# A Trainium2 encoder block: the softmax's sums of exponentials as products of f16 halves instead of fp32

## The chip, the cores and the metric

The kernel runs on one core of a Trainium2 chip. A core has five engines, each with its own instruction queue worked off in order: TensorE (PE; its weight loads are listed apart as PEld), VectorE (DVE), ScalarE (ACT), GpSimd (POOL) and SyncE (SP, which only issues DMAs). They share SBUF; TensorE's products go to PSUM, which POOL does not reach. The metric is the device time of one execution, in microseconds.

## What is computed

One layer of an encoder block, on two batches of 2048 tokens with 1024 features and the same weights. The part that matters here is the attention: 8 query heads in 2 groups (kv heads), head size 64, every query against all 2048 keys.

```python
def one_block(qblk):
    s = jnp.einsum('bkgqd,bskd->bkgqs', qblk, k).astype(jnp.float32) * scale
    pr = jax.nn.softmax(s, axis=-1).astype(v.dtype)
    return jnp.einsum('bkgqs,bskd->bqkgd', pr, v)
...
a = _blocked_gqa(q, k, v) * jax.nn.silu(ga)
fo = _fourier_branch(f, w_fmix) * jax.nn.silu(gf)
h = h + jnp.concatenate([a, fo], axis=-1) @ w_out
gate = jax.nn.sigmoid(_rmsnorm(h, g_ple) @ w_ple_gate)
return h + (p @ w_ple) * gate
```

The softmax is done as exponentials of the scores less their maximum, summed over the keys; the products with V are divided by the sums at the end.

## The kernel before

**Stages.** First the projections of both batches (until about 820 us of the profiled span), then a long stage in which attention and a filler run interleaved (until about 2592 us), then what is left of the filler. The filler is the Fourier branch and after it the output projection, the gate and the final norm of tile after tile of 128 tokens.

**Units and steps.** Attention goes by 64 units: one of two batches, one of two kv heads, one of 16 blocks of 128 queries. The four heads of a kv head and 128 queries make 512 columns. A unit has 8 steps, each with 256 of the 2048 keys. Step `g` belongs to unit `g // 8`, and `j = g % 8` is its number in the unit. In a step:

- `scores(u, j)` issues six f16 products (L1166) into two PSUM banks `ps_s` that the unit keeps, two more in its first step, and then two exponentials on ACT (L1169) into the tile `p` of the tag `p32`, of which there are seven buffers. POOL adds `p` to the running sum `acc` of the unit (L1172 at step 1, L1174 at steps 2 to 7): 128x1024 in fp32. At step 7 POOL folds the two halves of `acc` into one of 128x512 (L1176).
- `lead(g)` issues the products for the row maxima of a unit that comes later (L1193, into the one buffer of `ps_m`) and their reduction on DVE (L1201); at every step 3 also `nm` on ACT (L1211).
- At step 4, `sums(u - 1, ...)` sums the folded `acc` of the unit before over its partitions, by products with a tile of ones on PE (L1244): two fp32 products of 256 columns, side by side in the two column halves of the array. `divide` then takes the reciprocal in PSUM (L1251) and multiplies (L1252) on DVE.
- At steps 0 and 4, behind all that, `pv` issues the fp32 products of four steps' exponentials with V (L1229). A step with such products gets no filler work; every other step gets about as much as a budget allows.

**Order.** PE, ACT, DVE and SP work in the order in which the program issues (`manual_schedule`); the order on POOL is planned by the framework, with its own costs. What is given to `defer` is issued at the start of the next step, in `flush`, ahead of that step's scores and reductions; other filler work is issued where it stands, at the end of its step. So the filler's DVE work of step 3 (such as L1407, which adds a product in PSUM to `h`) comes ahead of what was deferred in step 3, and that ahead of the reduction of step 4:

```python
self.flush()
u, j = g // 8, g % 8
...
    scores(u, j)
self.drain(lead(g))
if j == 4:
    ...
        sums(u - 1, ps[:, 0:256])
        divide(u - 1, ps[:, 0:256])
```

The filler's lines that the prediction names: L1481 (its products, two halves of the rows side by side), L1407, L1531 and L1535 (the two f16 halves `h_hl` of the normalised rows, by ACT and then by DVE), L1502 (squares), and the `rsh` chains (an inverse square root by tiny instructions, mostly on POOL). L390 and L393 are the two f16 halves of a weight, by ACT and DVE, in the first stage. L1051 is in the Fourier branch.

Of the kernel before, what the change touches and what calls it, by code (L numbers as in the profile page):

```python
# [11 lines left out]
F16 = mybir.dt.float16  # L12
I32 = mybir.dt.int32
AF = mybir.ActivationFunctionType
ALU = mybir.AluOpType
# [23 lines left out]
FIRST, SLOW = 30, 0.85  # L39
LAG = 3  # L40
P32 = 7
WHOLE = 2 * NT - 2
STOPS = (6, 9, 12, 15, 18)
MB = 2
# [96 lines left out]
class Build:  # L141
# [848 lines left out]
    def fourier2(self, pool, hook):  # L990
# [82 lines left out]
        for t in range(16):  # L1073
            if t == 10:
# [4 lines left out]
            fT = (pool.tile([128, 4, 2, 128], F32, name="fT", bufs=2) if t >= FP else  # L1079
                  self.att.tile([128, 4, 2, 128], F32, name="fT", tag="p32", bufs=P32))  # L1080
            fx = None
# [42 lines left out]
    def attention(self, kvp):  # L1124
# [3 lines left out]
        nc, st = self.nc, self.st  # L1128
        units = self.unit_order()
        n = len(units)  # L1130
        last = {units[u][:2]: u for u in range(n)}
        kt, vt, Q, P, O, MX, ACC, AT, M4, S, MR = {}, {}, {}, {}, {}, {}, {}, {}, {}, {}, {}

        def load_kv(s, kv):
            for b in range(2):
                k = kvp.tile([128, 4, 3, 128], F16, name=f"k{kv}", bufs=2)
                for h in range(2):
                    nc.sync.dma_start(k[:, 2 * h:2 * h + 2], self.kTd[s][kv][:, 4 * b + 2 * h:4 * b + 2 * h + 2])
                kt[s, kv, b] = k
            for b in range(2):  # L1140
                v = kvp.tile([128, 8, 64], F32, name=f"v{kv}", bufs=2)
                nc.sync.dma_start(v[:], self.vd[s][kv][:, 8 * b:8 * b + 8])
                vt[s, kv, b] = v

        def load_q(u):
            s, kv, t = units[u]
            q1, q2 = [(pool if u > 2 else kvp).tile([128, 4, 128], F16, name=f"q{b}" if u > 2 else f"q{b}_0",
                                                    bufs=3) for b in (1, 2)]
            src = self.qTd[s][t][:, 4 * kv:4 * kv + 4, :]
            for b, q in enumerate((q1, q2)):  # L1150
                for y in range(2):
                    nc.sync.dma_start(q[64 * y:64 * y + 64], src[64 * b:64 * b + 64])
            Q[u] = q1, q2

        def scores(u, j):
            s, kv, t = units[u]
            P[u, j] = p = pool.tile([128, 2, 512], F32, name="p32", bufs=P32)
            k = kt[s, kv, j // 4]
            todo = [] if j else [(kone, MR.pop(u))]
            todo += [(k[:, j % 4, y], Q[u][b]) for y, b in ((1, 0), (1, 1), (2, 0))]  # L1160
            if j == 0:
                S[u] = [self.psS.tile([128, 512], F32, name="ps_s") for e in range(2)]
            for i, (w, q) in enumerate(todo):
                for e in range(2):
                    sl = slice(64 * e, 64 * e + 64)
                    nc.tensor.matmul(S[u][e][:], w[sl], q[sl].rearrange("p h q -> p (h q)"), start=j == i == 0,  # L1166
                                     stop=i + 1 == len(todo), skip_group_check=True)
            for e in range(2):
                nc.scalar.activation(p[:, e, :], S[u][e][:], AF.Exp, scale=self.sc["s_scale"][:])  # L1169
            if j == 1:  # L1170
                ACC[u] = pool.tile([128, 2, 512], F32, name="acc", bufs=2)
                nc.gpsimd.tensor_tensor(out=ACC[u][:], in0=P[u, 0][:], in1=p[:], op=ALU.add)  # L1172
            elif j > 1:
                nc.gpsimd.tensor_tensor(out=ACC[u][:], in0=ACC[u][:], in1=p[:], op=ALU.add)  # L1174
            if j == 7:
                nc.gpsimd.tensor_tensor(out=ACC[u][:, 0, :], in0=ACC[u][:, 0, :], in1=ACC[u][:, 1, :], op=ALU.add)  # L1176
                del Q[u], S[u]
                if u == last[s, kv]:
                    for b in range(2):
                        del kt[s, kv, b]  # L1180

        def maxima(u, k, first=False):

            s, kv, t = units[u]
            h, half = k // 2, k % 2
            if first:
                ps = [self.psX.tile([128, 512], F32, name="ps_x")[:] for _ in range(2)]
            else:
                pm = self.psM.tile([128, 1024], F32, name="ps_m")
                ps = [pm[:, c * 512:(c + 1) * 512] for c in range(2)]  # L1190
            for c in range(2):
                sl = slice(64 * c, 64 * c + 64)
                nc.tensor.matmul(ps[c], Q[u][0][sl, h, :], kt[s, kv, half][sl, :, 0, :], start=True, stop=True)  # L1193
            if k == 0:
                MX[u] = st.tile([128, 4, 2, 2 if first else 1], F32, name="a_mx", tag=f"a_mx{int(first)}", bufs=2)
                if first:
                    nc.gpsimd.memset(MX[u][:], -3e38)
            if first:
                yield
            for c, x in enumerate(ps if first else [pm[:]]):  # L1200
                nc.vector.reduce_max(MX[u][:, h, half, c:c + 1], x, axis=AX.X)  # L1201
            if k < 7:
                return
            mx = MX.pop(u)
            m = st.tile([128, 4], F32, name="a_m4", bufs=2)
            nc.vector.tensor_reduce(out=m[:], in_=mx[:].rearrange("p h a b -> p h (a b)"), op=ALU.max, axis=AX.X)
            M4[u] = m

        def negate(u):
            m = M4.pop(u)  # L1210
            nc.scalar.activation(nm[:].rearrange("p h (e c) -> p e h c", e=2)[:, :, :, 0],  # L1211
                                 m[:].unsqueeze(1).to_broadcast([128, 2, 4]), AF.Copy, scale=-1.0 / K_ONE)

        def max_rows(u):

            MR[u] = mr = kvp.tile([128, 4, 128], F16, name="mr", bufs=1)
            nc.sync.dma_start_transpose(mr[:], nm[:].rearrange("p h c -> p (h c)"))
# [20 lines left out]

        def sums(u, ps):

            acc = ACC.pop(u)
            av = acc[:, 0, :].rearrange("p (c e q) -> p e c q", e=2, q=128)
            for e in range(2):
                nc.tensor.matmul(ps[64 * e:64 * e + 64], self.ones[:], av[:, e], start=True, stop=True)  # L1244

        def divide(u, r):

# [21 lines left out]
        def lead(g):  # L1269

            v, k = divmod(g + AHEAD, 8)
            if v < n:
                yield from maxima(v, k, g < 0)
            if k == 1 and 0 <= v - 1 < n:
                negate(v - 1)
# [11 lines left out]
        pool = yield  # L1287
        self.ones = pool.tile([128, 64], F32, name="ones", bufs=1)
        nc.gpsimd.memset(self.ones[:], 1.0)
        fresh = {last[0, kv]: kv for kv in range(2)}  # L1290
        for g in range(8 * n + 7):
            self.step = g
            self.flush()
            u, j = g // 8, g % 8
            if j == 0 and 0 < u and u + 2 < n:
                load_q(u + 2)
            if j == 4 and u - 1 in fresh:
                load_kv(1, fresh[u - 1])
            if 0 <= u < n:
                scores(u, j)  # L1300
            self.drain(lead(g))
            if j == 4:
                if u + 1 < n:
                    max_rows(u + 1)
                if u > 0:
                    ps = self.bank()
                    sums(u - 1, ps[:, 0:256])
                    divide(u - 1, ps[:, 0:256])
            heavy = (g - 1) % PVG == PVG - 1 and 0 <= g - 1 < 8 * n
            if heavy:  # L1310
                self.run_slow(1 if j else 2)
                pv((g - 1) // 8, (g - 1) % 8 - PVG + 1)
            yield 0 if heavy else RATE if g >= 8 * n // 2 else 1 if g > FIRST else SLOW
# [39 lines left out]
    def outp(self, pool0, ow, open_pool):  # L1353
# [208 lines left out]
        def along(g, pr):  # L1562

            for us in g:
                for _ in range(round(us / 0.648) if us else 0):
                    next(pr, None)
                poll()
                yield us
# [59 lines left out]
        for t in range(N2 + 2):  # L1628
            pr = prep(t + 1) if ok(t + 1) else iter(())
            if ok(t):  # L1630
                yield from along(slot(out1(t, 0), t >= WHOLE), pr)
                if t == 1:
                    yield from middle(0)
                yield from along(slot(out1(t, 1), t >= WHOLE), pr)
                load_p(t)
                M.pop(t)
            if ok(t - 1):
                yield from wait(tk, t - 1)
                yield from along(slot(out3(t - 1, 0), t >= WHOLE), pr)
            if t:  # L1640
                yield from middle(t)
            if ok(t - 1):
                yield from along(slot(out3(t - 1, 1), t >= WHOLE), pr)
            if ok(t + 1):
# [226 lines left out]
```

## Time and profile before

| | |
|---|---|
| median of 3 runs | 2668.47 us (2668.46 to 2668.82) |
| the profiled execution: time, span | 2671.73 us, 2670.0 us |
| PE busy | 2611.3 us (98%) |
| DVE, ACT, POOL busy | 1612.9 (60%), 1184.7 (44%), 1630.1 us (61%) |
| granted TensorE clock, mean | 0.995 |
| the sums (L1244): records, mean of one | 256, 404 to 405 ns |
| POOL's adds (L1174): number, mean of one | 384, 2394 ns |

The profile shows one execution. A busy share is the time in which an engine had an instruction under way. A matrix product in fp32 stands in the profile as two records. In a list of one line's instructions, three numbers with strokes between them are the shortest, the median and the longest duration in ns. A time in brackets behind a row of a timeline is the idle time of that engine ahead of it, with what ended it.

### The profile page before, as it was taken

What the parts mean: (1) busy time and instruction counts of PE and PEld (TensorE: products, weight loads), DVE (VectorE), ACT (ScalarE), POOL (GpSimd) and SP (SyncE); (2) the same over time, 40 slices, a digit from 0 to 9 for tenths busy, and PEclk for the clock granted to TensorE, in tenths of its full rate; (3) what the DMA queues carried; (4) which work ended last, traced back from release to release, by engine and by line L of the source; (5) the groups of instructions that cost most, each with busy time, mean ns of one, the idle gap of its engine ahead of it and who ended that gap; (6) DMA issues with size and microseconds to landing.
All of it is one profiled execution on the core that took longest, in us unless ns stands there. A gap on an engine that the chain in (4) does not pass through costs nothing.

```text
span 2670.0 us, 49974 instructions
## 1 busy us (share of the span) xinstructions
PE 2611.3 (98%) x20096; PEld 1400.3 (52%) x20096; DVE 1612.9 (60%) x2300; ACT 1184.7 (44%) x1983; POOL 1630.1 (61%) x1376
## 2 busy tenths in 40 slices
PE   6999999999999999999999999999999999999998
PEld 3565655655556654545555544545544544555443
DVE  7756465565555775565675666665665666556634
ACT  4443243433224554544444544445445444544442
POOL 1233342333336885877877877877777877777760
PEclk9999999999999999999999999999999999999999
DMA  8567576676538772222222223322232332232223
GB/s 251 150 163 202 165 217 178 172 185 154 141 74 257 231 219 72 62 77 62 75 67 59 66 69 97 99 64 70 64 90 60 79 77 70 69 79 76 62 76 73
DMA packets 453386, 305.37 MB, mean 114 GB/s; under 512 B 294273, under 2 KB 394817, under 8 KB 453153
## 3 DMA queue, kind: packets, MB, share of 16 engines
q1 hardware_dynamic: 440240, 260.41, 37.9%
q0 software_dynamic: 12912, 41.77, 4.2%
q8 instruction: 157, 2.57, 0.4%
q14 instruction: 77, 0.62, 0.1%
HBM read 149.50 MB, written 86.51 MB: 88 GB/s over the span
## 4 chain that ended last, share of the span: by engine, by line
PE 49%; DVE 2%; ACT 1%; issue 0%; DMA 0%; DVEq 0%; SPq 0%; ACTq 0%
PE ps_g L1481 19%; PE ps_o L1229 12%; PE ps_s L1166 10%; PE ps_m L1193 3%; PE ps_f L451 3%; PE ps_x L451 2%; PE ps_f L1244 1%; DVE h L1521 0%; DVE a_mx L1201 0%; PE ps_g L451 0%; ACT p L1169 0%; DVE h_hl L1535 0%; ACT sq L1502 0%; DVE ps_f L1429 0%; ACT h_hl L1502 0%
## 5 line engine op out<-in xcount | busy, mean ns | idle before, releaser
L1174 POOL TENSOR_TENSOR acc<-acc,p 128x1024 f32<-128x1024 f32 x384 | 919.4, 2394 | 201.0 <-ACT p L1169 161.5
L1201 DVE TENSOR_REDUCE a_mx<-ps_m 128x1 f32<-128x1024 f32 x498 | 609.2, 1223 | 564.5 <-PE ps_m L1193 555.2
L1169 ACT ACTIVATE p<-ps_s,s_scale 128x512 f32<-128x512 f32 x1024 | 647.3, 684 | 652.6 <-PE ps_s L1166 634.9
L1481 PE MATMUL ps_g<-w_pg,hT 64*128 64x512 f16 x2784 | 492.2, 376 | 1.9 <-DVE h L1407 1.1
L1229 PE MATMUL ps_o<-p,v 128*64 128x256 f32 x4096 | 468.2, 381 | 0.0
L451 PEld LDWEIGHTS <-uc 128*128 128x128 f16 x3072 | 301.7, 98 | 310.0 <-issue 20.4
L1166 PE MATMUL ps_s<-q,k 64*128 64x512 f16 x3072 | 433.0, 378 | 6.1 <-ACT p L1169 5.9
L1229 PEld LDWEIGHTS ps_o<-p,v 128*64 128x64 f32 x4096 | 288.8, 137 | 166.7 <-issue 28.5
L1481 PEld LDWEIGHTS <-hT 64*128 64x128 f16 x2784 | 205.0, 94 | 155.4 <-issue 12.4
L1481 PE MATMUL ps_g<-w_wo,mh 64*128 64x512 f16 x1440 | 259.0, 376 | 1.2 <-DVE seen L1447 1.2
L1481 PE MATMUL ps_g<-w_wo,mT 64*128 64x512 f16 x1440 | 256.2, 376 | 0.0
L1166 PEld LDWEIGHTS <-k 64*128 64x128 f16 x3072 | 150.7, 94 | 200.7 <-issue 76.8
L1193 PE MATMUL ps_m<-k,q 64*128 64x512 f16 x996 | 199.9, 377 | 5.1 <-DVE a_mx L1201 4.8
L1172 POOL TENSOR_TENSOR acc<-p,p 128x1024 f32<-128x1024 f32 x64 | 150.7, 2355 | 64.2 <-ACT p L1169 63.6
L451 PEld LDWEIGHTS <-w_ga 128*128 128x128 f16 x1536 | 148.8, 98 | 33.6 <-issue 11.1
L942 POOL DMA_DIRECT2D gfd<-gt x32 | 19.7, 614 | 223.3 <-DVE gt L970 190.1
L1481 PEld LDWEIGHTS <-mh 64*128 64x128 f16 x1440 | 99.8, 94 | 91.2 <-issue 18.4
L1481 PEld LDWEIGHTS <-mT 64*128 64x128 f16 x1440 | 102.7, 94 | 81.3 <-issue 3.8
L1251 DVE RECIPROCAL ps_f<-ps_f 128x256 f32<-128x256 f32 x63 | 110.6, 1756 | 21.2 <-PE ps_f L1244 21.2
L451 PE MATMUL ps_x<-w_f,uc 128*128 128x512 f16 x480 | 105.9, 379 | 0.0
L451 PE MATMUL ps_x<-uc,w_ga 128*128 128x256 f16 x936 | 105.5, 273 | 0.0
L1236 ACT ACTIVATE at<-ps_o,a_scale 128x256 f32<-128x256 f32 x64 | 30.3, 473 | 167.5 <-PE ps_o L1229 167.5
(326 smaller groups left out, 3182.8 us busy)
## 6 DMA issues: line engine op xcount, KB each, us to landing
q<-qTd SPq DMA_DIRECT2D x256, 64.0 KB, 2.3
ag<-agd SPq DMA_DIRECT2D x64, 256.0 KB, 3.3
out<-h POOLq DMA_DIRECT2D x31, 512.0 KB, 3.0
x<-in_x_prompt SPq DMA_DIRECT2D x16, 512.0 KB, 5.2
gfd<-gt POOLq DMA_DIRECT2D x32, 256.0 KB, 2.6
gd<-ge POOLq DMA_DIRECT2D x32, 256.0 KB, 2.8
w_st<-in_w_out SPq DMA_DIRECT2D x32, 256.0 KB, 3.8
agd<-gat POOLq DMA_DIRECT2D x64, 128.0 KB, 2.8
```

The source lines that it names most:

```text
L451: self.nc.tensor.matmul(ps, lhs(ia, k), rhs(ib, k), start=(i == 0), stop=(i == 3 * ks - 1))
L1166: nc.tensor.matmul(S[u][e][:], w[sl], q[sl].rearrange("p h q -> p (h q)"), start=j == i == 0, stop=i + 1 == len(todo), skip_group_check=True)
L1169: nc.scalar.activation(p[:, e, :], S[u][e][:], AF.Exp, scale=self.sc["s_scale"][:])
L1172: nc.gpsimd.tensor_tensor(out=ACC[u][:], in0=P[u, 0][:], in1=p[:], op=ALU.add)
L1174: nc.gpsimd.tensor_tensor(out=ACC[u][:], in0=ACC[u][:], in1=p[:], op=ALU.add)
L1193: nc.tensor.matmul(ps[c], Q[u][0][sl, h, :], kt[s, kv, half][sl, :, 0, :], start=True, stop=True)
L1201: nc.vector.reduce_max(MX[u][:, h, half, c:c + 1], x, axis=AX.X)
L1229: nc.tensor.matmul(o[64 * f:64 * f + 64], vt[s, kv, c // 8][:, c % 8, :], p[:, e, f], start=(c == 0), stop=(c == 15))
L1236: nc.scalar.activation(at[:].rearrange("p c q -> p (c q)"), o, AF.Copy, scale=self.sc["a_scale"][:])
L1244: nc.tensor.matmul(ps[64 * e:64 * e + 64], self.ones[:], av[:, e], start=True, stop=True)
L1251: nc.vector.reciprocal(r, r)
L1481: nc.tensor.matmul(g[0][:], g[1](ia, k)[sl], g[2](ib, k)[sl], start=a, stop=z, skip_group_check=True)
```

## The change

The folded sum `acc` of the unit before (128x512, fp32) is split at step 3 into two f16 tiles: ACT copies it to f16, and DVE, through `defer`, subtracts that copy from `acc` and writes the rest as f16. Both halves lie in one tile `acc_h`, which takes a place of the tag `p32`. At step 4 the sums are then four f16 products with a tile of f16 ones, two per half, in place of the two fp32 ones. The fp32 ones stay, since `mix` uses them too.

```diff
--- before.py
+++ after.py
@@ -39,6 +39,7 @@
 FIRST, SLOW = 30, 0.85
 LAG = 3
 P32 = 7
+HALVE = 3
 WHOLE = 2 * NT - 2
 STOPS = (6, 9, 12, 15, 18)
 MB = 2
@@ -1129,7 +1130,7 @@
         units = self.unit_order()
         n = len(units)
         last = {units[u][:2]: u for u in range(n)}
-        kt, vt, Q, P, O, MX, ACC, AT, M4, S, MR = {}, {}, {}, {}, {}, {}, {}, {}, {}, {}, {}
+        kt, vt, Q, P, O, MX, ACC, AT, M4, S, MR, AR = ({} for _ in range(12))
 
         def load_kv(s, kv):
             for b in range(2):
@@ -1238,10 +1239,11 @@
 
         def sums(u, ps):
 
-            acc = ACC.pop(u)
-            av = acc[:, 0, :].rearrange("p (c e q) -> p e c q", e=2, q=128)
-            for e in range(2):
-                nc.tensor.matmul(ps[64 * e:64 * e + 64], self.ones[:], av[:, e], start=True, stop=True)
+            acc = AR.pop(u)
+            for b in range(2):
+                av = acc[:, b, :].rearrange("p (c e q) -> p e c q", e=2, q=128)
+                for e in range(2):
+                    nc.tensor.matmul(ps[64 * e:64 * e + 64], self.ones16[:], av[:, e], start=b == 0, stop=b == 1)
 
         def divide(u, r):
 
@@ -1287,6 +1289,8 @@
         pool = yield
         self.ones = pool.tile([128, 64], F32, name="ones", bufs=1)
         nc.gpsimd.memset(self.ones[:], 1.0)
+        self.ones16 = pool.tile([128, 64], F16, name="ones16", bufs=1)
+        nc.gpsimd.memset(self.ones16[:], 1.0)
         fresh = {last[0, kv]: kv for kv in range(2)}
         for g in range(8 * n + 7):
             self.step = g
@@ -1299,6 +1303,12 @@
             if 0 <= u < n:
                 scores(u, j)
             self.drain(lead(g))
+            if j == HALVE and u > 0:
+                acc, AR[u - 1] = ACC.pop(u - 1), pool.tile([128, 2, 512], F16, name="acc_h", tag="p32", bufs=P32)
+                nc.scalar.activation(AR[u - 1][:, 0, :], acc[:, 0, :], AF.Copy)
+                self.defer(lambda acc=acc, r=AR[u - 1]: nc.vector.tensor_tensor(
+                    out=r[:, 1, :], in0=acc[:, 0, :], in1=r[:, 0, :], op=ALU.subtract))
+                del acc
             if j == 4:
                 if u + 1 < n:
                     max_rows(u + 1)
```

## The prediction

> **What bounds the kernel now.** I read the page's busy shares first, then the busy time by stretch, then the chain that ended last, and at last the timelines of the four engines around one sum of exponentials.
>
> ```profile
> span 2670.0 us, 49974 instructions
> PE 2611.3 (98%) x20096; PEld 1400.3 (52%) x20096; DVE 1612.9 (60%) x2300; ACT 1184.7 (44%) x1983; POOL 1630.1 (61%) x1376
> PEclk9999999999999999999999999999999999999999
> ...
> PE ps_g L1481 19%; PE ps_o L1229 12%; PE ps_s L1166 10%; PE ps_m L1193 3%; PE ps_f L451 3%; PE ps_x L451 2%; PE ps_f L1244 1%; DVE h L1521 0%; DVE a_mx L1201 0%; PE ps_g L451 0%; ACT p L1169 0%; DVE h_hl L1535 0%; ACT sq L1502 0%; DVE ps_f L1429 0%; ACT h_hl L1502 0%
> ```
>
> ```profile
> 865.50:2591.60 1726.10, 1709.90 (x14755) 876.82 (x14753) 1062.68 (x1031) 846.58 (x1391) 1328.95 (x1074) 1.00 0.32 84
> ```
>
> The second fence is the stretch from the first sum to the last: 1726.10 us long, then the busy time of PE, PEld, DVE, ACT and POOL, the granted clock (1.00), the DMA share and GB/s. PE is busy for 1709.90 of it, so TensorE's order of work sets the time, and a wait put into it is paid nearly in full. POOL is busy for 1328.95 us, 77%. On the chain the sums (L1244) have 1%.
>
> The steps around the sum at 1523.39, PE first, then ACT, DVE and POOL (start, duration, engine, line; in brackets the idle time before and what ended it):
>
> ```profile
> 1520.06 0.87 PE L1166 MATMUL ps_s<-q,k 64*128 64x512 f16 x6
> 1520.71 0.43 PE L1193 MATMUL ps_m<-k,q 64*128 64x512 f16 x2
> 1521.12 1.47 PE L1481 MATMUL ps_g<-w_pg,hT 64*128 64x512 f16 x12
> 1522.41 0.83 PE L1166 MATMUL ps_s<-q,k 64*128 64x512 f16 x6
> 1523.06 0.40 PE L1193 MATMUL ps_m<-k,q 64*128 64x512 f16 x2
> 1523.39 0.65 PE L1244 MATMUL ps_f<-acc,ones 128*64 128x256 f32 x4
> 1523.87 3.62 PE L1229 MATMUL ps_o<-p,v 128*64 128x256 f32 x32
> 1527.43 0.82 PE L1166 MATMUL ps_s<-q,k 64*128 64x512 f16 x6
> ```
>
> ```profile
> 1520.96 1.26 ACT L1169 ACTIVATE p<-ps_s,s_scale 128x512 f32<-128x512 f32 x2 [2.19 <-PE ps_s L1166]
> 1522.12 0.23 ACT L1211 ACTIVATE nm<-a_m 128x8 f16<-128x8 f32 x1
> 1522.22 1.05 ACT L1502 ACTIVATE sq<-h 128x1024 f16<-128x1024 f32 x1
> ```
>
> ```profile
> 1521.18 1.22 DVE L1201 TENSOR_REDUCE a_mx<-ps_m 128x1 f32<-128x1024 f32 x1
> 1523.49 1.23 DVE L1201 TENSOR_REDUCE a_mx<-ps_m 128x1 f32<-128x1024 f32 x1 [1.09 <-PE ps_m L1193]
> ```
>
> ```profile
> 1522.37 2.37 POOL L1174 TENSOR_TENSOR acc<-acc,p 128x1024 f32<-128x1024 f32 x1 [0.90 <-ACT p L1169]
> ```
>
> Step 3 of the unit begins at 1520.06, step 4 at 1522.41. The last exponential of step 3 ends at 1522.22, 1.17 us before the sums. The add that reads it starts on POOL 0.15 us later and holds POOL until 1524.74.
>
> **The change part by part. PE.** The two fp32 products of a unit are four records; 0.48 us pass from their start to that of the product with V (1523.39 to 1523.87). A small part of that is entering the other tile shape, which the product with V pays as well where no sum precedes it; the sums' own part goes by L1229, 32 records in 3.56 us, 0.22 per pair of records, 0.44 in all. Of an f16 product with 256 columns the trace has only whole-array ones:
>
> ```profile
> L451 PE MATMUL ps_x<-uc,w_ga 128*128 128x256 f16 x936 | 105.5, 273 | 0.0
> ```
>
> 105.5 us over 936 is 0.113 us each. Two column halves ran side by side in fp32, so a pair should take about 0.11 and the two pairs 0.22 instead of 0.44; if the halves did not overlap, 0.45 and nothing gained. I take the overlap, as the nearest rows (L1244, L1229) show it. For going on to fp32 behind f16 no row in one tile shape stands by; between 0 and 0.11 us (1523.06 to 1523.39 is 0.33, where such a pair takes 0.22 as the three of L1166 from 1522.41 to 1523.06 do) I take 0.05, the middle. With no wait a unit gains 0.48 - 0.27, or 0.21 us, and 64 units 14 us.
> The Trainium skill, "TensorEngine Tiling (Array Packing)", Key Properties, says that a change of the tiling mode drains TensorE. By it the step from f16 to fp32, one mode, would be free, and the sum below 3 us less; no row here shows that step.
>
> **ACT.** 64 copies of 128x512 to f16. The rows of a like copy and of a like difference:
>
> ```profile
> L390 ACT ACTIVATE w_o<-w_st,w_wo_s 128x512 f16<-128x512 f32 x16 | 11.3, 722 | 25.5 <-DMA w_st<-in_w_out 19.1 <-DVE w_wo_i L279 3.2 <-DVE rsq_t L249 3.0
> L393 DVE SCALAR_TENSOR_TENSOR w_o<-w_st,w_gs,w_o 128x512 f16<-128x512 f32 x16 | 11.8, 748 | 10.2 <-ACT w_o L390 8.3 <-DMA agd<-gat 1.9
> ```
>
> ACT gets 64 x 0.72 = 46 us. Behind the copy stand the filler's work of step 3 and the exponentials of step 4; the scores of step 5, which need those, come only after the product with V (1523.87 to 1527.43), which covers it: nothing. The copy itself waits for the fold on POOL (L1176), which over all units ends 3.1 us or more before the sums and 1.5 us or more before the copy: nothing. In this unit the copy starts behind nm at about 1522.22 and ends at 1522.94.
>
> **DVE.** The difference is put off to the start of step 4, so it is queued on DVE behind all that step 3 issued, and ahead of the reduction of step 4. Here DVE is free from 1522.40. Alone it takes 0.69 to 0.75 us: 0.69 for a tensor_tensor (L1051 below, one input in PSUM), 0.75 by L393. It would be done at about 1523.66, and the second pair, which needs it, would start some 0.2 us late. But it reads both inputs from SBUF while POOL adds. What the trace shows of that:
>
> ```profile
> 1192.80 3.05 DVE L1535 SCALAR_TENSOR_TENSOR h_hl<-h,h_r,h_hl 128x1024 f16<-128x1024 f32 x1
> ...
> 1189.96 4.80 POOL L1174 TENSOR_TENSOR acc<-acc,p 128x1024 f32<-128x1024 f32 x2
> 1194.84 2.13 POOL L1176 TENSOR_TENSOR acc<-acc 128x512 f32<-128x512 f32 x1
> ...
> L1535 DVE SCALAR_TENSOR_TENSOR h_hl<-h,h_r,h_hl x32: 1277/1730/3049, 1047.1 to 2640.0; 128x1024 f16<-128x1024 f32 x32
> L1252 DVE TENSOR_TENSOR at<-at,ps_f x63: 420/421/422, 868.6 to 2594.2; 128x256 f32<-128x256 f32 x63
> L1176 POOL TENSOR_TENSOR acc<-acc x64: 1263/1272/2301, 855.1 to 2584.1; 128x512 f32<-128x512 f32 x64
> L1051 DVE TENSOR_TENSOR fo<-ps_g,fo x22: 677/692/693, 848.5 to 974.8; 128x512 f32<-128x512 f32 x22
> ```
>
> L1535, f32 and f16 in from SBUF as the new difference, takes 1.28 us at best and 3.05 at 1192.80: it ends at 1195.85, 1.09 after POOL's add ended at 1194.76, and POOL's fold right behind it takes 2.13 instead of 1.27. One waits for the other to end. L1252 and L1051, with an input in PSUM, never vary beyond 16 ns. So the difference has to wait for the add that runs: in this unit until 1524.74, and then its work without the start-up, about 0.55 (0.69 less the 0.14 to 0.2 that lie inside the wait, L1535: 1.28 less 1.09).
> The Trainium skill states this rule in "SBUF — State Buffer", section "SBUF: two separate sides": a VectorE instruction with two SBUF inputs and a GpSimd one share a port pair, held for a whole instruction, the loser blocked. By that rule, the trace agrees (3.05 us), this change pays for every sum beside an add; without it the sum would be that of the second rival.
>
> **The wait on PE.** Difference done at 1525.29; 0.05 us to PE (below, DVE's reduction ends at 1048.91 + 1.22 = 1050.13 and PE starts at 1050.18); second pair 0.11, step to fp32 0.05: the product with V starts at 1525.50 instead of 1523.87, 1.63 us late. Behind the waiting sums stand this product and the scores of step 5, so PE has nothing else to do; reduction and reciprocal on DVE go later by less than the product's 3.6 us, and POOL's next add 0.55 later with 23% idle.
>
> **The sum.** I read the 63 units that have a step 4 of a next unit in the same way. The last exponential of step 3 ends 1.00 to 3.05 us ahead of the sums, 1.61 in the mean. In 33 units POOL starts that add within 0.4 us of it; 32 of them lose 1.28 us each, 40.9 us. In the other 30 POOL is late with an earlier add, or in the chain of tiny rsh instructions, between which the difference slips in; they lose 0.52 each, 15.7 us (nine gain 0.2). The first of the 63 (sums at 865.51) and the last (2569.77):
>
> ```profile
> 862.93 1.26 ACT L1169 ACTIVATE p<-ps_s,s_scale 128x512 f32<-128x512 f32 x2
> 863.20 4.79 POOL L1174 TENSOR_TENSOR acc<-acc,p 128x1024 f32<-128x1024 f32 x2
> ...
> 2566.83 7.24 POOL L1174 TENSOR_TENSOR acc<-acc,p 128x1024 f32<-128x1024 f32 x3
> 2569.77 0.65 PE L1244 MATMUL ps_f<-acc,ones 128*64 128x256 f32 x4
> ```
>
> In the first a lagging add ends at 865.55 and the loss is 0.3; in the last one ends at 2569.19, and the unit gains. The 33rd prompt unit is apart. Sums at 1043.38, and DVE still has step 3's work ahead of the reduction, so ahead of the difference too:
>
> ```profile
> 1047.05 1.28 DVE L1535 SCALAR_TENSOR_TENSOR h_hl<-h,h_r,h_hl 128x1024 f16<-128x1024 f32 x1 [1.28 <-ACT h_hl L1531]
> 1048.25 0.75 DVE L1407 SCALAR_TENSOR_TENSOR h<-ps_g,mixo,h 128x512 f32<-128x512 f32 x1
> 1048.91 1.22 DVE L1201 TENSOR_REDUCE a_mx<-ps_m 128x1 f32<-128x1024 f32 x1
> ...
> 1050.18 0.39 PE L1193 MATMUL ps_m<-k,q 64*128 64x512 f16 x2 [1.16 <-DVE a_mx L1201]
> 1051.74 0.39 PE L1481 MATMUL ps_g<-w_pg,hT 64*128 64x512 f16 x1 [0.73 <-DMA hT<-h_hl]
> ```
>
> The difference starts at 1048.94, behind another add until 1050.66: PE waits some 7.5 us, and its old waits there (1.16, 0.73 and small ones, 2.2) go. 5.3 us lost, once.
>
> 40.9 + 15.7 + 5.3 = 61.9 us. Against the profiled execution (2671.73, span 2670.0) that is 2733.6; it stands 3.3 above the median of the runs, 2668.47, so the forecast in the median's terms is 2730.
>
> **Edits at nothing.** acc_h takes a place among the seven of p32, so exponentials reuse one six steps back instead of seven: the nearest one (step 6, p of step 0) comes behind scores queued on PE after the product that frees it, 2 steps later, and POOL's add of step 0 is 5 steps old. A gain is excluded. The second memset is one instruction before the stage. The bias in mix still uses the fp32 ones.
>
> **The rivals.**
> - *No wait for POOL, DVE alone on time.* The difference takes 0.69 us wherever it falls. Then 22 units with a late exponential or a busy DVE lose 0.16 to 1.0 and 32 gain 0.15 to 0.22; read per unit this nets -0.9 us, and with the 5.3 us of the odd unit the time is 2673, inside 0.2%. For it: L1535 is as short as 1.28. Against it: its median is 1.73. It decides if a tensor_tensor with f16 output doesn't wait as L1535 does. Chance 0.06.
> - *The change does what it says: faster.* The difference is always done before the second pair, so the full 14 us come in: 2655. It needs POOL's add to end 0.6 us ahead of the sums; the add starts 0.15 us after an exponential that ends 1.61 ahead, and takes 2.36. That holds for nine units. Chance 0.06, mostly for POOL's order being planned anew around the new work.
> - *Two adds deep.* POOL's queued next add goes first whenever it is ready; one more 2.37 us in each of the 63 units, 149 us: 2880. Against it: at 1194.76 DVE went ahead of the waiting fold. Chance 0.03.
> - *POOL never late.* PE's waits give POOL time; with every add 0.15 us behind its exponential the units lose 73 us and the odd one 5.3: 2747. This is the upper side of the forecast's own case, as is a first pair that waits for the difference too (0.11 x 55 units, 6 us more).
>
> **How the numbers follow.** Forecast case 0.85, rivals 0.06, 0.06 and 0.03. The range: below, the 30 late units lose nothing (-15.7), the step to fp32 is free (-3) and up to 8 us of old waits of PE are absorbed, 2703; above, POOL never late with both pairs waiting, 2753. I take 2703 to 2755. A measurement of this kernel tells about 0.2%, 5.3 us, from no change. Slower 0.88, same 0.06, faster 0.06.
>
> **What would show it.** PE's idle time before the second pair of a sum should name the difference on DVE as its releaser, in some 50 units, with a mean near 1.2 us. The difference should have a minimum of 0.69 and a median near 2 us, ending 0.5 us after an add. The four f16 records should lie within 0.25 us where nothing waits. Wrong would be: differences all near 0.7 us, or POOL in another order, its add of step 3 behind the difference.

## The result, and the profile after

| | median | lowest to highest |
|---|---|---|
| before (5 runs) | 2668.47 us | 2668.21 to 2672.59 |
| changed (5 runs) | 2746.39 us | 2742.28 to 2749.55 |

The ratio is 1.0287, with a 95% interval of 1.0273 to 1.0301: slower by 78 us, where 62 were forecast (2730, range 2703 to 2755). The profiled execution took 2748.89 us; its span is 2747.1 us, against 2670.0 before.

Line numbers shift by one below line 40 and by ten below the change (L1201 is now L1202, L1407 is L1417, L1229 is L1230); the sums are L1246, the copy L1308, the difference L1309. From the page, the engines and the chain that ended last:

```profile
PE 2614.5 (95%) x20096; PEld 1421.0 (52%) x20096; DVE 1727.7 (63%) x2364; ACT 1214.5 (44%) x2047; POOL 1643.8 (60%) x1377
...
PE ps_g L1491 19%; PE ps_x L452 17%; PE ps_o L1230 16%; PE ps_s L1167 11%; PE ps_f L452 7%; PE ps_g L452 7%; DVE acc_h L1309 4%; PE ps_m L1194 3%; ACT p L1170 2%; DMA gf_in<-gfd 1%; DVE a_mx L1202 1%; ACT acc_h L1308 1%; PE ps_x L926 1%; PE ps_f L1246 1%; DVE w_mx L313 1%
```

PE is busy for about as long as before (2614.5 against 2611.3 us) in a span 77 us longer, and VectorE's difference has come onto the chain with 4%. The waits, and the instructions of the tile `acc_h` (shortest, median and longest in ns):

```profile
PE ps_f L1246 <- DVE acc_h L1309: 72.0, 48, 7.6
...
L1308 ACT ACTIVATE acc_h<-acc x64: 617/627/642, 865.0 to 2666.4; 128x512 f16<-128x512 f32 x64
L1309 DVE TENSOR_TENSOR acc_h<-acc,acc_h x64: 682/2391/2852, 865.8 to 2667.0; 128x512 f16<-128x512 f32 x64
```

PE waited 72.0 us for the difference ahead of 48 sums, and 1.4 us ahead of one more, whose tile is named `ps_g`: 73.4 in all. The difference takes 0.68 us at its shortest and 2.39 in the median. One unit in the timelines, PE, ACT, DVE, POOL:

```profile
1109.61 0.43 PE L1194 MATMUL ps_m<-k,q 64*128 64x512 f16 x2
1109.97 0.30 PE L1246 MATMUL ps_f<-acc_h,ones 128*64 128x256 f16 x2
1112.07 0.33 PE L1246 MATMUL ps_f<-acc_h,ones 128*64 128x256 f16 x2 [1.79 <-DVE acc_h L1309]
1112.18 5.12 PE L1230 MATMUL ps_o<-p,v 128*64 128x256 f32 x30
...
1108.96 0.63 ACT L1308 ACTIVATE acc_h<-acc 128x512 f16<-128x512 f32 x1
...
1109.62 2.39 DVE L1309 TENSOR_TENSOR acc_h<-acc,acc_h 128x512 f16<-128x512 f32 x1 [0.53 <-ACT acc_h L1308]
...
1109.12 2.35 POOL L1175 TENSOR_TENSOR acc<-acc,p 128x1024 f32<-128x1024 f32 x1 [1.17 <-ACT nm L1212]
```

POOL's add of step 3 runs from 1109.12 to 1111.47. The difference begins 0.5 us into it and ends at 1112.01, 0.54 after it; the second pair of the sum waits 1.79 us. The whole trace shows the same: 51 of the 64 differences began while such an add ran, and each of them ended 0.55 us after the end of that add. The last row of PE shows something else: thirty records of the product with V take 5.12 us, where 32 took 3.62 before. The busy time by stretch (PE, PEld, DVE, ACT, POOL, then the granted clock), for three stretches of 3.4 us:

```profile
1108.79:1112.20 3.41, 1.62 (x17) 0.73 (x15) 2.88 (x3) 2.99 (x6) 2.63 (x2) 1.00 0.13 25
1112.20:1115.60 3.40, 3.40 (x19) 2.32 (x19) 3.37 (x4) 0.00 (x0) 2.07 (x1) 0.50 0.29 57
1115.60:1119.00 3.40, 3.40 (x34) 1.90 (x32) 1.35 (x2) 0.64 (x2) 0.00 (x0) 1.00 0.24 50
```

In the stretch with the wait PE was busy for 1.62 of 3.41 us; through the next its granted clock was 0.50. That costs 1.7 us more. In the attention it happens seven times for 3.4 us and once for 6.8, against twice for 3.4 before; in the first half of the 6.8 PE was waiting anyway.

**Where the 77 us are.** Taken unit by unit from the timelines of PE: from the maxima's products ahead of a sum to the product with V, 64 units took 50.6 us before and 118.2 after, 67.6 more. That is more than the waits of 73.4 less the gain (64 times 0.24, below), because a wait is counted only from the modelled end of the first pair: at 1109.97 the second pair starts 2.10 us after the first, where 0.13 pass without a wait, and only 1.79 of the 1.96 lost stand as idle time. All that lies between the units took 8.8 more. In the stretches at half clock PE worked for 27.0 us after and 6.6 before; half of that is lost, 13.5 against 3.3, so the clock costs about 10 us more, and some old waits went. After, the slow stretches fell nearly all on the product with V, whose busy time grew by 13.0 us (the first row is the kernel before); before, more than half of them fell on other products. The rest is 0.8, at the start.

```profile
L1229 PE MATMUL ps_o<-p,v 128*64 128x256 f32 x4096 | 468.2, 381 | 0.0
...
L1230 PE MATMUL ps_o<-p,v 128*64 128x256 f32 x4096 | 481.2, 388 | 0.0
```

### The profile page after: what moved, and what is told of

Read it like the earlier page. It is cut to its first block, busy times and chain, and to the rows that moved or that the text cites. A ratio compares the mean times of both kernels' runs of the same rounds, so it can differ in the third digit from the quotient of the medians.

```text
span 2747.1 us, 50114 instructions
## 1 busy us (share of the span) xinstructions
PE 2614.5 (95%) x20096; PEld 1421.0 (52%) x20096; DVE 1727.7 (63%) x2364; ACT 1214.5 (44%) x2047; POOL 1643.8 (60%) x1377
## 4 chain that ended last, share of the span: by engine, by line
PE 82%; DVE 9%; ACT 4%; DMA 2%; issue 2%; SPq 0%; POOL 0%; ACTq 0%; DVEq 0%; POOLq 0%
PE ps_g L1491 19%; PE ps_x L452 17%; PE ps_o L1230 16%; PE ps_s L1167 11%; PE ps_f L452 7%; PE ps_g L452 7%; DVE acc_h L1309 4%; PE ps_m L1194 3%; ACT p L1170 2%; DMA gf_in<-gfd 1%; DVE a_mx L1202 1%; ACT acc_h L1308 1%; PE ps_x L926 1%; PE ps_f L1246 1%; DVE w_mx L313 1%
## 5 line engine op out<-in xcount | busy, mean ns | idle before, releaser
L1202 DVE TENSOR_REDUCE a_mx<-ps_m 128x1 f32<-128x1024 f32 x498 | 608.5, 1222 | 508.2 <-PE ps_m L1194 499.8
L1230 PE MATMUL ps_o<-p,v 128*64 128x256 f32 x4096 | 481.2, 388 | 0.0
L1230 PEld LDWEIGHTS ps_o<-p,v 128*64 128x64 f32 x4096 | 312.4, 140 | 144.1 <-issue 28.1
L452 PEld LDWEIGHTS <-w_ga 128*128 128x128 f16 x1536 | 148.8, 98 | 33.3 <-issue 11.1
L1309 DVE TENSOR_TENSOR acc_h<-acc,acc_h 128x512 f16<-128x512 f32 x64 | 127.8, 1997 | 37.9 <-ACT acc_h L1308 37.6
```

The lines of the kernel that those rows point to most:

```text
L452: self.nc.tensor.matmul(ps, lhs(ia, k), rhs(ib, k), start=(i == 0), stop=(i == 3 * ks - 1))
L1230: nc.tensor.matmul(o[64 * f:64 * f + 64], vt[s, kv, c // 8][:, c % 8, :], p[:, e, f], start=(c == 0), stop=(c == 15))
L1309: self.defer(lambda acc=acc, r=AR[u - 1]: nc.vector.tensor_tensor(out=r[:, 1, :], in0=acc[:, 0, :], in1=r[:, 0, :], op=ALU.subtract))
```

## The experiments

Two theories stood against each other beside the rivals of the prediction. The port theory: the difference has two SBUF inputs and waits until POOL's running instruction ends, and PE waits for it. The load theory: 64 copies and 64 differences slow the filler on ACT and DVE, wherever the sums stand; a variant of it is that the difference is late by its own length. All ratios are to the kernel before on the same chip (medians of 2670.16 to 2671.54 us there; 2668.47 for the changed kernel), with 95% intervals. Line numbers differ a little from run to run.

| run | time, us | ratio | PE's wait for the difference, us |
|---|---|---|---|
| the changed kernel | 2746.39 | 1.0287 [1.0273, 1.0301] | 73.4 |
| no_diff | 2655.95 | 0.9948 [0.9934, 0.9963] | - |
| dead_halves | 2685.52 | 1.0061 [1.0044, 1.0078] | - |
| swap_adds | 2681.78 | 1.0043 [1.0028, 1.0058] | 13.7 |
| split_adds | 2679.88 | 1.0030 [1.0018, 1.0042] | 19.4 |
| before_split | 2665.66 | 0.9984 [0.9975, 0.9993] | - |
| behind_pv | 2701.80 | 1.0118 [1.0103, 1.0133] | 4.1 |
| step2 | 2686.70 | 1.0061 [1.0044, 1.0078] | 0 |
| step2_swap | 2691.05 | 1.0075 [1.0060, 1.0090] | 0 |
| keep_busy | 2742.66 | 1.0271 [1.0256, 1.0287] | 36.0 |
| pool_halves | 2667.46 | 0.9990 [0.9981, 0.9999] | - |
| fold16 | 2651.23 | 0.9929 [0.9914, 0.9944] | - |
| fold16_split | 2648.33 | 0.9912 [0.9895, 0.9929] | - |

**Without the difference (no_diff).** The second pair reads the first half again, so the sums come out about twice as large as they should be, and what the kernel returns is not the layer; only its time is of use.

```diff
-                av = acc[:, b, :].rearrange("p (c e q) -> p e c q", e=2, q=128)
+                av = acc[:, 0, :].rearrange("p (c e q) -> p e c q", e=2, q=128)
...
-                self.defer(lambda acc=acc, r=AR[u - 1]: nc.vector.tensor_tensor(
-                    out=r[:, 1, :], in0=acc[:, 0, :], in1=r[:, 0, :], op=ALU.subtract))
```

> The changed kernel without VectorE's difference: the second pair of each sum reads the first half again, so the low halves are left out of the result. Port theory: nothing waits any more, 64 times 0.24 us are saved: 2651 to 2656 us, two or three half-clock stretches in the attention. Load theory: ScalarE's copies alone keep the time above 2668 us.

2655.95 us: TensorE's saving is real, and 64 copies on ACT cost nothing that shows. So the loss is the difference's, not the copies'. (The expectation says that the low halves are left out; the high halves are also counted twice.)

**The same work, read by nobody (dead_halves).** The sums are the fp32 ones again.

```diff
-            acc = AR.pop(u)
...
+            AR.pop(u)
+            acc = ACC.pop(u)
+            av = acc[:, 0, :].rearrange("p (c e q) -> p e c q", e=2, q=128)
+            for e in range(2):
+                nc.tensor.matmul(ps[64 * e:64 * e + 64], self.ones[:], av[:, e], start=True, stop=True)
...
-                acc, AR[u - 1] = ACC.pop(u - 1), pool.tile([128, 2, 512], F16, name="acc_h", tag="p32", bufs=P32)
+                acc, AR[u - 1] = ACC[u - 1], pool.tile([128, 2, 512], F16, name="acc_h", tag="p32", bufs=P32)
```

> The kernel before with the copy and the difference made as in the changed kernel, but read by nobody: the sums are the fp32 ones. Port theory (what costs is TensorE's wait in front of the sums): the difference is as long (median near 2.4 us), but only the reduction behind it is late, which the product with V covers: 2669 to 2676 us. Load theory (the new work on ScalarE and VectorE, and POOL's held-up adds, cost by themselves): above 2700 us.

2685.52 us, above the port theory's range and far below the load theory's. The difference is as long as in the changed kernel (median 2394 ns), and PE's wait in front of the sums is gone, but holding VectorE does cost something:

```profile
PE ps_m L1193 <- DVE a_mx L1201: 4.8, 9, 1.3
...
PE ps_m L1194 <- DVE a_mx L1202: 14.9, 17, 3.4
```

The maxima's products waited 4.8 us for the reductions in the kernel before (first row), now 14.9: I had supposed that the product with V covers a late reduction everywhere, and it does not. Two more half-clock stretches of 3.4 us came with it. Held VectorE work alone thus costs 15 us (2685.52 against 2670.50 on this chip), and most of the 78 us hang on PE's wait for the difference.

**POOL's add out of the way (swap_adds).** As many adds as before; that of step 3 is issued behind that of step 4.

```diff
-            elif j > 1:
-                nc.gpsimd.tensor_tensor(out=ACC[u][:], in0=ACC[u][:], in1=p[:], op=ALU.add)
+            elif j > 1 and j != 3:
+                for x in (p, P[u, 3]) if j == 4 else (p,):
+                    nc.gpsimd.tensor_tensor(out=ACC[u][:], in0=ACC[u][:], in1=x[:], op=ALU.add)
```

> The changed kernel with POOL's add of step 3 put behind its add of step 4, so that POOL waits for the exponentials of step 4 just when the difference runs; as many adds as before. Port theory: the difference's median falls from 2.39 to near 0.7 us, the wait at the sums from 73 us to under 25, time 2672 to 2690 us. Rival (the difference is late by its own length behind exponential and copy, POOL has no part): the same as the changed kernel, 2740 to 2750 us.

```profile
1104.56 0.69 DVE L1310 TENSOR_TENSOR acc_h<-acc,acc_h 128x512 f16<-128x512 f32 x1 [0.52 <-ACT acc_h L1309]
...
1106.86 2.36 POOL L1176 TENSOR_TENSOR acc<-acc,p 128x1024 f32<-128x1024 f32 x1 [3.78 <-ACT p L1170]
...
L1310 DVE TENSOR_TENSOR acc_h<-acc,acc_h x64: 678/693/2870, 867.3 to 2602.2; 128x512 f16<-128x512 f32 x64
```

In the unit shown POOL is idle until 1106.86, and the difference is done in 0.69 us at 1105.25. The same instruction at the same place, with POOL idle throughout in 36 of the 64 units, takes 0.693 us in the median instead of 2.391; the wait falls from 73 to 13.7 us, the time to 2681.78 us. The rival "late by its own length" is out; POOL's add is the cause.

**Adds in halves (split_adds), and the control (before_split).**

```diff
             elif j > 1:
-                nc.gpsimd.tensor_tensor(out=ACC[u][:], in0=ACC[u][:], in1=p[:], op=ALU.add)
+                for e in range(2):
+                    nc.gpsimd.tensor_tensor(out=ACC[u][:, e], in0=ACC[u][:, e], in1=p[:, e], op=ALU.add)
```

> The changed kernel with each of POOL's adds of steps 2 to 7 in two halves of 128x512, about 1.2 us each in place of one of 2.36. Port theory: the difference waits for half an add at most, if it goes ahead of the second half as it went ahead of a queued fold: its longest falls from 2.85 to about 1.8 us, the wait of the sums from 73 to 15 to 35 us, time 2672 to 2700 us. Rival (POOL's next half goes first, or the difference is late by itself): 2735 to 2755 us.

> The kernel before with POOL's adds in halves, as a control for the run split_adds. Port theory: only the filler's own differences with two SBUF inputs wait less, and the waits they cause on TensorE were few: 2664 to 2672 us. If the halves by themselves cost (more instructions on POOL): above 2676 us.

```profile
L1310 DVE TENSOR_TENSOR acc_h<-acc,acc_h x64: 679/856/1793, 865.2 to 2598.0; 128x512 f16<-128x512 f32 x64
```

A blocking instruction of half the length makes half the delay: the longest difference is 1.79 us, as expected, and the kernel comes to 2679.88. The control is at 0.9984: the shorter adds help the kernel before a little too. The filler has differences with two SBUF inputs of its own, `mh` and `h_hl`, and they take 46.7 and 52.4 us in all where they took 52.1 and 57.3; that the gain comes from them was not tried.

**More time for the difference: sums behind the product with V (behind_pv), copy a step earlier (step2).**

```diff
-                if u > 0:
-                    ps = self.bank()
-                    sums(u - 1, ps[:, 0:256])
-                    divide(u - 1, ps[:, 0:256])
...
                 pv((g - 1) // 8, (g - 1) % 8 - PVG + 1)
+            if j == 4 and u > 0:
+                ps = self.bank()
+                sums(u - 1, ps[:, 0:256])
+                divide(u - 1, ps[:, 0:256])
```

> The changed kernel with the sums and the division issued behind the product with V of step 4 instead of ahead of it, so that the difference has 3.6 us more. Port theory (the difference on VectorE waits until POOL's running add ends, and TensorE waits for it ahead of the sums): nearly every difference is done in time, each of the 64 units saves the 0.24 us that the undisturbed units of the changed kernel show, TensorE's half-clock stretches in the attention fall back to two or three: 2653 to 2660 us. Load theory (46 us more on ScalarE and 128 on VectorE slow the filler, wherever the sums stand): still above 2700 us.

2701.80 us: the port theory's range is missed by over 40 us, and the time lies where the load theory put it, though the trace gives another reason. The wait for the difference is down to the 4.1 us of one unit, but the division moved too, which I had overlooked. A unit on DVE, with PE behind it:

```profile
1538.97 2.40 DVE L1309 TENSOR_TENSOR acc_h<-acc,acc_h 128x512 f16<-128x512 f32 x1 [0.47 <-ACT acc_h L1308]
1541.30 1.21 DVE L1202 TENSOR_REDUCE a_mx<-ps_m 128x1 f32<-128x1024 f32 x1
...
1543.63 1.75 DVE L1253 RECIPROCAL ps_f<-ps_f 128x256 f32<-128x256 f32 x1
1545.41 0.42 DVE L1254 TENSOR_TENSOR at<-at,ps_f 128x256 f32<-128x256 f32 x1
1545.75 1.22 DVE L1202 TENSOR_REDUCE a_mx<-ps_m 128x1 f32<-128x1024 f32 x1
...
1547.02 0.39 PE L1194 MATMUL ps_m<-k,q 64*128 64x512 f16 x2 [0.68 <-DVE a_mx L1202]
```

The reciprocal cannot start before the sums, which now come after the product with V; the reduction of step 5 is queued behind it, and the maxima's products of step 6 wait for that. Their waits for reductions come to 36.7 us, 31.8 of them at step 6, against 4.8 before. The wait changed its place.

> The changed kernel with the copy at step 2 instead of 3 (HALVE = 2), the sums where they were. Port theory: the sums find the difference done, but a difference that waits for POOL's add of step 2 now stands ahead of VectorE's reduction of step 3, for which the maxima's products of step 4 wait: about 21 us by the trace of before, less 15 gained: 2665 to 2685 us. Rival (late by its own length alone): a whole step more is enough for everything, 2651 to 2658 us.

2686.70 us (the edit is HALVE = 2), within 2 us of the port theory's range, and almost 29 above the rival's. No sum waits, but the reduction of step 3 stands behind a blocked difference (median 2338 ns), and 22.6 of the following 31.5 us are waits at step 4:

```profile
PE ps_m L1194 <- DVE a_mx L1202: 31.5, 30, 2.4
```

**Both edits for step 2 (step2_swap).** HALVE = 2 and POOL's add of step 2 issued behind that of step 3.

> The copy at step 2 and POOL's add of step 2 put behind its add of step 3, so that the difference runs while POOL waits for the exponentials of step 3, and a step ahead of the sums. Port theory: the difference's median is 0.69 us, the reduction of step 3 is no longer held up (31.5 us of waits of the maxima's products at HALVE = 2), 2655 to 2665 us. Rival (VectorE's queue is the trouble even with a short difference): as at HALVE = 2, 2680 to 2690 us.

2691.05 us: the expectation failed. The difference is short (median 693 ns), yet the maxima's products still wait 26.9 us. One such place, on DVE and POOL:

```profile
2121.44 3.26 DVE L1402 SCALAR_TENSOR_TENSOR mh<-ag,mix_s,mh 128x1024 f16<-128x1024 f32 x1
2124.62 1.21 DVE L1203 TENSOR_REDUCE a_mx<-ps_m 128x1 f32<-128x1024 f32 x1
...
2118.84 4.78 POOL L1176 TENSOR_TENSOR acc<-acc,p 128x1024 f32<-128x1024 f32 x2
```

Here it is `mh`, a difference of the filler with two SBUF inputs, that waits for POOL until 2123.62 and takes 3.26 us instead of 1.28; over all 32 it takes 73.8 us where it took 52.1 before, and the filler's other one (`h_hl`) 70.0 for 57.3. The adds were moved out of one difference's way and into another's; how much of the loss that makes was not tried.

**The clock by itself (keep_busy).** Products that nobody reads, ahead of the sums:

```diff
+            for i in range(6):
+                av = acc[:, 0, :].rearrange("p (c e q) -> p e c q", e=2, q=128)
+                for e in range(2):
+                    nc.tensor.matmul(self.spare[64 * e:64 * e + 64], self.ones16[:], av[:, e], start=True, stop=True)
             for b in range(2):
...
+                    self.spare = ps[:, 256:512]
```

> The changed kernel with six pairs of f16 products of the first half, written beside the sums and read by nobody, ahead of the sums, so that TensorE works for about 0.7 us of each wait for the difference. Clock theory (a wait of 1.8 us and more in one of the clock's 3.4 us stretches halves the clock for the next): the stretches at half clock in the attention fall from 8 to 3 or fewer, the product with V (L1230, mean 388 ns) goes back to 381, and the time falls to 2735 to 2744 us although nothing is taken away. Rival (the half-clock stretches come from something else, or the waits' own sum is all): 8 stretches again, 2746 to 2756 us.

```profile
L1230 PE MATMUL ps_o<-p,v 128*64 128x256 f32 x4096 | 470.9, 382 | 0.0
```

Three half-clock stretches in the attention instead of eight (a double one counted once), and the product with V is back at 382 ns. PE's wait for the difference falls from 73.4 to 36.0 us, because the added products run in it. That stretches with much waiting are followed by half clock is borne out; the time, 2742.66 us, lies in the range, but its ratio's interval overlaps that of the changed kernel, so that the net gain is not shown.

**Ways round the port (pool_halves, fold16, fold16_split).** First both halves on POOL, behind its fold, with nothing new on DVE:

```diff
+                acc, AR[u] = ACC.pop(u), pool.tile([128, 2, 512], F16, name="acc_h", tag="p32", bufs=P32)
+                nc.gpsimd.tensor_copy(AR[u][:, 0, :], acc[:, 0, :])
+                nc.gpsimd.tensor_tensor(out=AR[u][:, 1, :], in0=acc[:, 0, :], in1=AR[u][:, 0, :], op=ALU.subtract)
...
-            if j == HALVE and u > 0:
...
```

> Both halves made by POOL itself right behind its fold at step 7 (a copy to f16, then the difference), nothing on ScalarE and VectorE; sums at step 4 as f16. Port theory: POOL cannot block itself and VectorE has no work with two SBUF inputs here, so the sums find their halves done; POOL gets about 2.5 us more per unit of 27, and its longest lags (fold 3.1 us ahead of the sums) may cost a few us: 2652 to 2662 us, as without the difference (2656). Rival (POOL, now at 85%, becomes the wait): exponentials or sums wait for POOL, above 2670 us.

2667.46 us, ratio 0.9990: about as fast as before, and 5 us beyond the expected range. No sum waits for its halves, and PE waits no longer for exponentials than before, but the maxima's products wait 11.1 us for reductions. The filler's `mh` and `h_hl` took 59.3 and 64.7 us (52.1 and 57.3 before): with more work on POOL, VectorE's other differences take longer. The span is 9.7 us above that of no_diff; in the attention PE is idle for 6.1 us more and loses 3.1 us more to half clock, which is nearly all of it. That the longer differences make all of the idle time was not tried.

Then no halves at all: the fold writes f16, and the sums are a single pair, with nothing left at step 3. The low halves are left out, so the sums are made of terms rounded to f16, 11 bits.

```diff
-                nc.gpsimd.tensor_tensor(out=ACC[u][:, 0, :], in0=ACC[u][:, 0, :], in1=ACC[u][:, 1, :], op=ALU.add)
+                acc, AR[u] = ACC.pop(u), pool.tile([128, 1, 512], F16, name="acc_h", tag="p32", bufs=P32)
+                nc.gpsimd.tensor_tensor(out=AR[u][:, 0, :], in0=acc[:, 0, :], in1=acc[:, 1, :], op=ALU.add)
...
-            for b in range(2):
+            for b in range(1):
...
-            if j == HALVE and u > 0:
...
```

> POOL's fold writes f16 at once, and the sums are one pair of f16 products of it: no copy, no difference, the low halves are left out (the sums' partial terms are rounded to 11 bits). Port theory: nothing new stands on the shared port, TensorE saves 0.24 us and one more pair of 0.13 in each of 64 units, 24 us: 2643 to 2650 us. Rival (the saving on TensorE is given back elsewhere, as in the run pool_halves): 2655 to 2668 us.

> The run fold16 with POOL's adds in halves as well. Port theory: the sum of both effects, 2640 to 2650 us. If the halves cost on POOL: above 2652 us.

2651.23 and 2648.33 us; the first just above its range, the second, with POOL's adds in halves, inside. At 0.9912 it is the fastest version run: it gives PE the saving, puts no new instruction beside POOL's adds, and halves those adds, at the price of precision.

## Why the prediction was right, and where its size was off

- **Direction and mechanism: right.** VectorE's new instruction waits for POOL's running add and PE for it; swap_adds and split_adds show this by taking the add away and by halving it. Behind an add the difference ends 0.55 us after it, the figure that was taken. PE waited ahead of 49 sums, for 1.5 us in the mean, where some 50 and 1.2 were named. By the rule of the Trainium skill that the prediction cites ("SBUF — State Buffer", "SBUF: two separate sides": an exclusive port pair, held for the whole instruction) this is the expected delay.
- **The gain without a wait: nearly right.** 0.24 us per unit, where 0.21 was forecast. An undisturbed unit of the changed kernel shows it, from 1084.29 to 1084.53 instead of 0.48:

```profile
1084.29 0.41 PE L1246 MATMUL ps_f<-acc_h,ones 128*64 128x256 f16 x4
1084.53 0.81 PE L1230 MATMUL ps_o<-p,v 128*64 128x256 f32 x6
```

  The step from f16 to fp32 in one tile shape, put at 0.05 us, has hardly any room in these 0.24: two pairs at the 0.11 that was taken fill 0.22 of them. That is in line with what the prediction drew from the Trainium skill, "TensorEngine Tiling (Array Packing)", Key Properties, where a change of the tiling mode drains TensorE: the mode does not change here.
- **The waits at the sums: right in sum.** Forecast 40.9 + 15.7 + 7.5 = 64.1 us with the odd unit's wait; measured, as lengthening from the maxima's products to the product with V, 67.6. Of the same units the prompt ones gave 39.7, the late ones 20.6 (five more than forecast; why was not looked into), and the odd one 7.57:

```profile
1057.49 0.43 PE L1246 MATMUL ps_f<-acc_h,ones 128*64 128x256 f16 x2 [7.59 <-DVE acc_h L1309]
```

- **What was missing: the clock.** The prediction read a granted clock of 1.00 and gave no term for what PE's waits do to it. Six more half-clock stretches, one of them double, cost about 10 us (PE worked 27.0 us at half clock instead of 6.6), the largest part of the 16 by which the forecast was short; 3.5 us more lie in the units (67.6 for 64.1). The range held in part by luck: its upper end stood for a POOL that is never late, not for the clock.
- **"The product with V covers the late reduction": partly wrong.** dead_halves puts a price of 10 us of waits on what the prediction called covered. In the changed kernel these waits hardly grew (6.2 us, 4.8 before); that PE's own waits at the sums hid them there is likely, but was not tried.
- **The rivals.** "No wait for POOL" needed differences near 0.7 us; the median was 2.39. "The change does what it says" needed the difference done ahead of the second pair; in 49 sums it was not. "Two adds deep" is out as well: the longest was 2.85, one add of 2.36 and the difference's rest. "POOL never late" came a little true: 35 of 63 adds started within 0.4 us instead of 33.
- **Two slips in the text.** Without the port rule the sum would be that of the first rival in the list (no wait for POOL, 2673 us), not of the second, and 64 times 0.21 are 13.4 us, not 14. Neither changes the forecast.

## What to carry to other kernels

Before giving VectorE an instruction with two SBUF inputs, look at what POOL runs at that moment: its price is then the rest of POOL's instruction plus most of its own time (here 0.55 of 0.69 us), and everything queued behind it in VectorE's order pays too. Moving it or moving POOL's work may only shift the clash (step2, step2_swap), unless POOL is idle there (swap_adds); shorter POOL instructions lessen it (split_adds), and doing without the instruction removes it (fold16). An operation with no second SBUF input was not tried in its place. And a wait put into a busy TensorE can cost more than its own length, because the clock can fall for the stretch that follows.

## What the runs showed of the hardware that I had not expected

In the changed kernel a difference that began while POOL added ended 0.55 us after the add in all of 51 cases; with POOL idle (swap_adds) it took 0.69 in all.

A wait of 1.8 us was once enough to halve TensorE's clock for the next 3.4 us, where it fell into one of the stretches of 3.4 us in which the granted clock changes (busy 1.62 of 3.41 us at 1108.79). In the changed kernel's attention, all seven stretches with more than 1.9 us of idle time were followed by one at 0.50, of those with 1.78 to 1.86 two of eight, and below that none. The kernel before has exceptions: two stretches with 1.1 and 1.2 us were followed by half clock (988.62 and 1019.34, each with several waits of 0.2 to 0.6 us for exponentials and reductions), and one with 1.9 was not; step2_swap has another with 1.9 that was not, and one with 1.84 that was; in fold16_split three with 1.3 to 1.4 were, between 980 and 1050 us. What else counts beside idle time stays open.
